# Half of the experts of a product-key FFN by one fetch per token instead of dense products, on one Trainium2 core

## The chip, the cores and the metric

The kernel runs on one core of one Trainium2 chip. The metric is the device time of one execution in microseconds. TensorE (PE) multiplies, VectorE (DVE) and ScalarE (ACT) work on tiles, GpSimd (POOL) and SyncE (SP) issue most DMAs. TensorE writes into PSUM, eight banks of 512 fp32 columns for each of 128 partitions.

## The reference

One decoder layer on 256 tokens of 1024 features: a sparse-attention and convolution mixer with residual, then a retrieval FFN. Only the FFN (peer_ffn) is touched. For each token and each of 8 heads it makes a query of two halves, scores 128 keys with each half, takes the top 16 of both, adds them in pairs, takes the top 16 pairs and a softmax g over these. A pair (i, j) is expert i*128 + j, of 16384:

```
a = gelu(einsum('bqhkd,bqd->bqhk', peer_u[expert], h2))
out = einsum('bqhk,bqhkd->bqd', g * a, peer_v[expert])
```

So each token uses 128 experts, each one a row of 1024 numbers in peer_u and one in peer_v. The result times gate2 is added to the residual.

## The kernel before, in words

The first 195 us (conditioning, mixer, output projection, second norm) end in h2, transposed (features on partitions), as two parts h2h and h2l, whose sum is h2. `split` (L116) makes such parts of a tile: a rounded copy on ScalarE (L117) and the rest on VectorE (L118). `mm3` (L120) multiplies two split operands in three passes (L121 to L123).

All weights come as tiles of 128x1024 (512 KB) through one queue in the order of use: `load` (L110) issues the DMA on SyncE, `advance` (L141) splits the tile, except those whose number is in `FULL`, which stay whole and are multiplied unsplit; `fill` (L156) keeps two tiles ahead. Rows of the gate2 conditioning (w_ada, 5) are put between V tiles 16 to 72 (L336).

The FFN is dense in the experts. `retrieve` (L805) first makes the queries (16 tiles) and their scores, with `stage1` top-16 rounds between them, then pairs, top 16 and softmax. It is a generator: after each piece it yields a cost, and the loop over U tiles draws pieces up to `BUDGET` a tile (L1002). `u_tile` (L960) multiplies the 128 experts of one j with all 256 tokens (8 calls of mm3, 256 columns) and takes the gelu on ScalarE. The first 64 (J0) run beside `retrieve`. The next 64 run beside `g_tile` (L975): for four tokens a step, ScalarE makes a one-hot of i (L981, L984) and VectorE one of j times g (L982); their product on TensorE (L986) is the gate of each (i, j), which is multiplied into B (L993). Then 128 V tiles: B's tile for j (split, `wh` and `wl`) times the tile of V, 12 matmuls of 512 columns into four output banks (L1020); last, `finish` multiplies with gate2, adds the residual and stores.

In the FFN VectorE's order is the order written (`manual_schedule`, L998); the other engines' order is the scheduler's.

Of the kernel before, what the change touches and what calls it, by code (L numbers as in the profile page):

```python
# [21 lines left out]
H = 8  # L22
# [13 lines left out]
# Order of the work. Streamed tiles are counted in the order in which they are used.  # L36
# [10 lines left out]
J0 = 64  # L47


def layout(a):  # L50
    """Only moves data: transposes, slices and repeats of the inputs."""
# [31 lines left out]
    o["pu"] = a["peer_u"].reshape(128, 128, KD, 128).transpose(1, 3, 2, 0)  # L83
    o["pv"] = a["peer_v"].reshape(128, 128, D).transpose(1, 0, 2)
# [7 lines left out]
def body(tc, i, out):  # L92
# [8 lines left out]
    his = pool("his", 3)  # L101
    los = pool("los", 3)
# [38 lines left out]
    def advance():  # L141
        pump(1)
        raw, use = loaded.pop(0)
        if use is not None:
            use(raw)
            return
        count[0] += 1
        if count[0] in FULL:
            ahead.append((raw,))
            return  # L150
        hi = his.tile([128, D], F32R, name="hi")
        lo = los.tile([128, D], F32R, name="lo")
        split(hi, lo, raw)
        ahead.append((hi, lo))
# [89 lines left out]
    def fold(col, acc, g):  # L244
        """Adds the sums of half of acc over its partitions to a column vector."""
# [23 lines left out]
    def normed(tb):  # L269
        """x times its reciprocal root mean square, tokens on partitions."""  # L270
# [52 lines left out]
    W += [(i["pu"][j].rearrange("p k c -> p (k c)"), None) for j in range(NJ)]  # L323
# [12 lines left out]
    for j in range(NJ):  # L336
        if j >= 16 and j % 8 == 0 and j < 80:
            k = (j - 16) // 8
            queue.append((i["w_ada"][5, k], add_row(gate2, k)))
        queue.append((i["pv"][j], None))  # L340
# [454 lines left out]
    B0 = pool("B0").tile([128, NJ // 2, L], F32, name="B0")  # L795
    tr = pool("tr")
    gw = pool("gw", 2)
    Ti = tr.tile([128, L], F32, name="Ti")
    Tj = tr.tile([128, L], F32, name="Tj")
    Tg = tr.tile([128, L], F32, name="Tg")  # L800
    p2 = ExitStack()
    r1 = p2.enter_context(tc.tile_pool(name="r1", bufs=1))
    r2 = p2.enter_context(tc.tile_pool(name="r2", bufs=2))

    def retrieve():  # L805
        skT = r1.tile([128, 16, 128], F32, name="skT")
        nc.scalar.dma_start(out=skT, in_=i["sk"])
        v16 = [r1.tile([128, 16, 16], F32, name=f"v16{tb}") for tb in range(NT)]
        x16 = [r1.tile([128, 16, 16], U32, name=f"x16{tb}") for tb in range(NT)]

        def top16(items, tag):
            """items: (values, sorted values out, positions out); chains run side by side."""
            ws = []
            for c, v, x in items:
                nc.vector.max(out=v[:, 0:8], in_=c)
            yield 0.4
            for c, v, x in items:
                nc.vector.max_index(out=x[:, 0:8], in_max=v[:, 0:8], in_values=c)
            yield 0.4
            for n, (c, v, x) in enumerate(items):  # L820
                w = r2.tile([128, c.shape[-1]], F32, name=f"{tag}{n}")
                nc.vector.match_replace(out=w, in_to_replace=v[:, 0:8], in_values=c, imm_value=NEG)
                ws.append(w)
            yield 0.4
            for w, (c, v, x) in zip(ws, items):
                nc.vector.max(out=v[:, 8:16], in_=w)
            yield 0.4
            for w, (c, v, x) in zip(ws, items):
                nc.vector.max_index(out=x[:, 8:16], in_max=v[:, 8:16], in_values=w)
            yield 0.4  # L830

        def stage1(hp, sg):
            return top16([(sg[:, tb], v16[tb][:, hp], x16[tb][:, hp]) for tb in range(NT)], "wv")

        def ready():
            while todo:
                yield from stage1(*todo.pop(0))

        def scores(hp, pqT):
            ps = p_acc.tile([128, NT, 128], F32, name="acc")  # L840
            for tb in range(NT):
                nc.tensor.matmul(ps[:, tb], pqT[:, tb * 128:tb * 128 + 128], skT[:, hp], start=True, stop=True)  # L842
            sg = r2.tile([128, NT, 128], F32, name="sg", bufs=10)
            nc.scalar.copy(sg, ps)
            todo.append((hp, sg))

        todo = []
        prev = None
        cur = iter(())
# [23 lines left out]
        yield 0  # L873
        yield from cur
        yield from ready()
        TB = range(NT)
        vv = [v16[tb].rearrange("p (h z) k -> p h z k", z=2) for tb in TB]
        xf = [r1.tile([128, 16, 16], F32, name=f"xf{tb}") for tb in TB]
        xv = [z.rearrange("p (h z) k -> p h z k", z=2) for z in xf]
        for tb in TB:  # L880
            nc.vector.tensor_copy(xf[tb], x16[tb])
        for tb in TB:
            nc.vector.tensor_scalar(xv[tb][:, :, 0], xv[tb][:, :, 0], 128.0, None, op0=OP.mult)
        yield 1.2
        cv = [r1.tile([128, H, NC2], F32, name=f"cv{tb}") for tb in TB]
        ce = [r1.tile([128, H, NC2], F32, name=f"ce{tb}") for tb in TB]
        o = 0
        a = 0
        while a < 16:
            nb = PAIRS[a]  # L890
            na = 1
            while a + na < 16 and PAIRS[a + na] == nb:
                na += 1
            for tb in TB:
                for c, s in ((cv[tb], vv[tb]), (ce[tb], xv[tb])):
                    dst = c[:, :, o:o + na * nb]
                    if nb == 1:
                        in0 = s[:, :, 0, a:a + na]
                        in1 = s[:, :, 1, 0:1].to_broadcast([128, H, na])
                    elif na == 1:  # L900
                        in0 = s[:, :, 0, a:a + 1].to_broadcast([128, H, nb])
                        in1 = s[:, :, 1, 0:nb]
                    else:
                        dst = dst.rearrange("p h (a b) -> p h a b", b=nb)
                        in0 = s[:, :, 0, a:a + na, None].to_broadcast([128, H, na, nb])
                        in1 = s[:, :, 1, None, 0:nb].to_broadcast([128, H, na, nb])
                    nc.vector.tensor_tensor(dst, in0, in1, op=OP.add)
            o += na * nb
            a += na
            yield 0.5  # L910
        tv = [r1.tile([128, H, 16], F32, name=f"tv{tb}") for tb in TB]
        tx = [r1.tile([128, H, 16], U32, name=f"tx{tb}") for tb in TB]
        for h in range(H):
            yield from top16([(cv[tb][:, h], tv[tb][:, h], tx[tb][:, h]) for tb in TB], "wc")
        tf = [r1.tile([128, H, 16], F32, name=f"tf{tb}") for tb in TB]
        gg = [r1.tile([128, H, 16], F32, name=f"gg{tb}") for tb in TB]
        gs = [r1.tile([128, H], F32, name=f"gs{tb}") for tb in TB]
        ef = [r1.tile([128, H, 16], F32, name=f"ef{tb}") for tb in TB]
        for tb in TB:
            nc.vector.tensor_copy(tf[tb], tx[tb])  # L920
            nc.vector.tensor_tensor(gg[tb], tv[tb], tv[tb][:, :, 0:1].to_broadcast([128, H, 16]), op=OP.subtract)
            nc.scalar.activation(out=flat(gg[tb]), in_=flat(gg[tb]), func=AF.Exp)
        yield 0.6
        for tb in TB:
            for h in range(H):
                for k in range(16):
                    ju = r2.tile([128, NC2], F32, name="ju")
                    nc.vector.scalar_tensor_tensor(ju, iota[:, :NC2], tf[tb][:, h, k:k + 1], ce[tb][:, h],  # L928
                                                   op0=OP.is_equal, op1=OP.mult,
                                                   accum_out=ef[tb][:, h, k:k + 1])  # L930
                    if k % 2:
                        yield 0.37
            nc.vector.tensor_reduce(out=gs[tb], in_=gg[tb], axis=AX.X, op=OP.add)
# [68 lines left out]
    for j in range(J0):  # L1002
        u_tile(j, 0)
        left += BUDGET
        while left > 0:
            left -= next(gen, 99.0)
# [66 lines left out]
```

## Time and profile before

| | us |
|---|---|
| median of 3 runs (lowest, highest) | 1032.94 (1032.71, 1033.36) |
| span of the profiled execution | 1031.9 |
| TensorE busy | 991.0 |
| VectorE busy | 774.2 |
| ScalarE busy | 595.9 |
| moved by DMA | 191.82 MB |

The profiled execution has no time of its own besides its span, first to last instruction. Busy time of TensorE counts matmuls whose ends are modelled. An fp32 matmul that is not split shows as two records.

### The profile page before, as it was taken

The page shows a single profiled execution, that of the slowest core. Times are in us where ns is not written, and L with a number is a line of the kernel's source. Part 1 is how long each engine was busy: PE and PEld are TensorE (multiplying, and loading weights), DVE is VectorE, ACT ScalarE, POOL GpSimd, SP SyncE. Part 2 cuts the span into 40 slices and gives each one's busy share as a digit, 9 for nine tenths or more (in the row PEclk, how much of TensorE's full clock was granted, in tenths as well). Part 3 has the DMA queues.
Part 4 walks back from the last instruction along what each step waited for, and adds up shares of the span by engine and source line. Part 5 has one row for each costly group of instructions (what it writes and reads, how often), then busy time and mean ns, then how long its engine had stood idle before and what let it go on. Part 6 is the DMA issues. An engine that isn't in the chain of part 4 may idle for free.

```text
span 1031.9 us, 18401 instructions
## 1 busy us (share of the span) xinstructions
PE 991.0 (96%) x6642; PEld 912.4 (88%) x6642; DVE 774.2 (75%) x2103; ACT 595.9 (58%) x1210; POOL 7.5 (1%) x20
## 2 busy tenths in 40 slices
PE   2599989999999999999999999999999999999998
PEld 2599987899999999999999999988888888888886
DVE  5789687788988999777788888866666666665655
ACT  3354643545445454599888888845454455455452
POOL 1000000000000000000000000000000000000000
PEclk9799998999999999999999999999999999999999
DMA  9686486345655655544444444456677777665663
GB/s 317 223 311 222 171 277 211 98 144 155 181 183 176 190 180 185 184 144 134 141 138 143 144 143 136 136 180 207 214 216 218 210 223 222 202 189 180 198 191 121
DMA packets 52891, 191.82 MB, mean 186 GB/s; under 512 B 6112, under 2 KB 6144, under 8 KB 52672
## 3 DMA queue, kind: packets, MB, share of 16 engines
q1 hardware_dynamic: 52416, 189.30, 58.4%
q8 instruction: 52, 0.85, 0.3%
q10 hardware_dynamic: 144, 1.05, 0.3%
q0 software_dynamic: 240, 0.31, 0.1%
q14 instruction: 39, 0.32, 0.1%
HBM read 189.58 MB, written 1.05 MB: 185 GB/s over the span
## 4 chain that ended last, share of the span: by engine, by line
PE 93%; DVE 4%; DMA 1%; ACT 1%; issue 0%; SPq 0%; ACTq 0%; DVEq 0%
PE acc L121 14%; PE acc L123 14%; PE acc L122 14%; PE mm L121 13%; PE mm L122 13%; PE mm L123 13%; PE pg L986 6%; PE acc L632 2%; DMA raw<-in_w_ada_dram 1%; DVE gate L219 1%; PE acc L842 1%; PE pg L517 1%; DVE acc L219 0%; PE mm L708 0%; ACT hi L117 0%
## 5 line engine op out<-in xcount | busy, mean ns | idle before, releaser
L118 DVE TENSOR_TENSOR lo<-raw,hi 128x1024 fp32r<-128x1024 f32 x302 | 369.1, 1223 | 122.7 <-ACT hi L117 120.3
L117 ACT CAST hi<-raw 128x1024 fp32r<-128x1024 f32 x302 | 316.0, 1047 | 158.1 <-PE mm L122 105.3
L121 PE MATMUL mm<-h2h,hi 128*128 128x256 f32 x1152 | 333.0, 289 | 0.5 <-ACT hi L117 0.4
L122 PE MATMUL mm<-h2l,hi 128*128 128x256 f32 x1152 | 325.9, 283 | 0.0
L123 PE MATMUL mm<-h2h,lo 128*128 128x256 f32 x1152 | 325.8, 283 | 0.0
L121 PEld LDWEIGHTS mm<-h2h,hi 128*128 128x128 f32 x1152 | 220.7, 192 | 0.9 <-ACT hi L117 0.9
L122 PEld LDWEIGHTS mm<-h2l,hi 128*128 128x128 f32 x1152 | 221.0, 192 | 0.0
L123 PEld LDWEIGHTS mm<-h2h,lo 128*128 128x128 f32 x1152 | 220.5, 191 | 0.0
L121 PE MATMUL acc<-hi,wh 128*128 128x512 f32 x512 | 199.7, 390 | 0.0
L123 PE MATMUL acc<-hi,wl 128*128 128x512 f32 x512 | 199.3, 389 | 0.0
L122 PE MATMUL acc<-lo,wh 128*128 128x512 f32 x512 | 199.3, 389 | 0.0
L117 ACT CAST wh<-B 128x256 fp32r<-128x256 f32 x128 | 52.0, 407 | 148.4 <-PE acc L122 145.6
L122 PEld LDWEIGHTS acc<-lo,wh 128*128 128x128 f32 x512 | 96.1, 188 | 20.1 <-issue 0.2
L123 PEld LDWEIGHTS acc<-hi,wl 128*128 128x128 f32 x512 | 96.1, 188 | 20.0
L121 PEld LDWEIGHTS acc<-hi,wh 128*128 128x128 f32 x512 | 96.1, 188 | 20.0 <-issue 0.2
L118 DVE TENSOR_TENSOR wl<-B,wh 128x256 fp32r<-128x256 f32 x128 | 54.2, 424 | 52.4 <-ACT wh L117 51.8
L981 ACT ACTIVATE oi<-iota,Ti 128x128 f32<-128x128 f32 x256 | 88.0, 403 | 0.0
L993 DVE TENSOR_TENSOR B<-pg,B 128x256 f32<-128x256 f32 (+63 forms) x127 | 45.0, 355 | 46.3 <-PE pg L986 46.3
L982 DVE TENSOR_SCALAR oj<-iota,Tj,Tg 128x128 f32<-128x128 f32 x256 | 71.3, 342 | 1.6 <-PE pg L986 1.6
L986 PE MATMUL pg<-oj,oi 128*128 128x128 f32 x512 | 67.6, 275 | 0.0
L986 PEld LDWEIGHTS pg<-oj,oi 128*128 128x128 f32 x512 | 62.8, 192 | 0.0
L928 DVE SCALAR_TENSOR_TENSOR ju<-iota,tf,ce 128x50 f32<-128x50 f32 x256 | 51.7, 266 | 0.0
(220 smaller groups left out, 945.9 us busy)
## 6 DMA issues: line engine op xcount, KB each, us to landing
raw<-in_pu_dram SPq DMA_DIRECT2D x128, 512.0 KB, 3.7
raw<-in_pv_dram SPq DMA_DIRECT2D x128, 512.0 KB, 4.3
raw<-in_w_ada_dram SPq DMA_DIRECT2D x48, 512.0 KB, 5.0
raw<-in_wq_dram SPq DMA_DIRECT2D x16, 512.0 KB, 3.7
raw<-in_w_c_dram SPq DMA_DIRECT2D x12, 512.0 KB, 4.7
raw<-in_w_kv_dram SPq DMA_DIRECT2D x8, 512.0 KB, 5.9
raw<-in_w_out_dram SPq DMA_DIRECT2D x8, 512.0 KB, 5.0
raw<-in_w_iq_dram SPq DMA_DIRECT2D x4, 512.0 KB, 4.8
```

Source lines behind the costliest of these rows:

```text
L117: nc.scalar.copy(hi, src)
L118: nc.vector.tensor_tensor(lo, src, hi.bitcast(F32), op=OP.subtract)
L121: nc.tensor.matmul(ps, a[0], b[0], start=first, stop=False)
L122: nc.tensor.matmul(ps, a[0], b[1], start=False, stop=False)
L123: nc.tensor.matmul(ps, a[1], b[0], start=False, stop=last)
L219: nc.vector.scalar_tensor_tensor(acc[:, s], raw[:, s], sc[:, k:k + 1], acc[:, s], op0=OP.mult, op1=OP.add)
L632: nc.tensor.matmul(ps[0], w[0][:, s], hT[:, k], start=k == 0, stop=k == KD - 1)
L928: nc.vector.scalar_tensor_tensor(ju, iota[:, :NC2], tf[tb][:, h, k:k + 1], ce[tb][:, h], op0=OP.is_equal, op1=OP.mult, accum_out=ef[tb][:, ...
L981: nc.scalar.activation(out=oi[:, n], in_=iota, func=AF.Square, bias=Ti[:, t:t + 1])
L982: nc.vector.tensor_scalar(oj[:, n], iota, Tj[:, t:t + 1], Tg[:, t:t + 1], op0=OP.is_equal, op1=OP.mult)
L986: nc.tensor.matmul(ps[:, n], oi[:, n], oj[:, n], start=True, stop=True)
L993: nc.vector.tensor_tensor(B[:, :m, t], pv[:, j0:j0 + m], B[:, :m, t], op=OP.mult)
```

## The change

- The tiles of U and V for j < 64 stay dense, but whole (`WHOLE`): each product is one unsplit fp32 matmul, against h2f, the fp32 sum of h2h and h2l made on GpSimd. B keeps only j < 64, and the gate product has 64 columns.
- The experts with j >= 64 come by fetch: U and V rows lie side by side in one array `uv` (8 KB a row). For each token GpSimd issues one indirect DMA by the list of its 128 experts, into a buffer of 128 partitions; an index with j < 64 has 65536 added, is out of bounds and is not moved. Nine such buffers are there (`ring`): three share the pool of split weights, six are new.
- Tokens go in quads, one from each strip of 32 partitions. h2 is transposed back to rows (`rows_of_h2`), split. For a token a matmul over its strip of 32 rows (`tile_position`) with one column of the identity, repeated 128 times, spreads its row of h2 over 128 partitions in PSUM; VectorE multiplies it with the fetched U rows and sums (two tokens and half of the features a turn, four turns a quad). After gelu and gate, `strips` multiplies the four tokens' coefficients with the fetched V rows, in column strips of 32, into the same output banks as the dense V tiles. Then the next fetch is issued.
- The pieces are laid between the dense matmuls by `run`, a budget in us. Retrieval goes one block of 128 tokens at a time; the lookup of the expert is three operations on 16x50 elements in place of 256 small ones, with the middle one on GpSimd for the first block. `g_step` staggers the gate product over three tiles, and after the U tiles it runs on until all 64 groups are done.
- All engines' order is now the order written. The gate2 rows lie between U tiles 4 to 18.

```diff
+WHOLE = set(FULL) | set(range(53, 53 + 2 * J0))
+ROWS = tuple(range(4, 20, 2))
...
+    nc.gpsimd.tensor_tensor(h2f, h2h.bitcast(F32), h2l.bitcast(F32), op=OP.add)
...
+        for tb in TB:
+            for g in range(2):
+                pt = p_g.tile([128, 4, 128], F32, name="pg")
+                for z in range(4):
+                    nc.tensor.transpose(pt[:, z], h2f[:, g * 4 + z, TS[tb]], ident)
+                s = slice(g * 512, g * 512 + 512)
+                split(h2r[0][:, tb, s], h2r[1][:, tb, s], flat(pt))
...
+    def stream():
+        yield from cur
+        while todo:
+            yield from stage1(*todo.pop(0))
+        yield from retrieve(0)
+        yield from retrieve(1)
+        state["R"] = True
+        yield 0.1
+        yield from pairs()
...
+    def run(us):
+        spent[0] += us
+        while spent[0] > 0:
+            z = next(gen, None)
+            if z is None:
+                spent[0] = 0.0
+                return
+            spent[0] -= z
...
+        for k in range(KD):
+            nc.tensor.matmul(ps, w[0][:, k * 128:k * 128 + 128], h2f[:, k], start=k == 0, stop=k == KD - 1)
+            if k % 4 == 3:
+                run(1.75)
...
+    def ring():
+        n = state["row"] = state.get("row", -1) + 1
+        if n % RINGS == 0:
+            return halves.tile([128, 2 * D], F32, name="uv", tag="hl")
+        return uvp.tile([128, 2 * D], F32, name="uv")
...
+    def fetch():
+        n = state["quad"] = state.get("quad", -1) + 1
+        if n >= L // 4:
+            return
+        rows = []
+        for q in range(4):
+            t = n // 32 * 128 + q * 32 + n % 32
+            rows.append(ring())
+            nc.gpsimd.indirect_dma_start(
+                out=rows[q], out_offset=None, in_=i["uv"],
+                in_offset=bass.IndirectOffsetOnAxis(ap=iv[:, t:t + 1], axis=0),
+                bounds_check=128 * 128 - 1, oob_is_err=False)
+        quads.append(rows)
+
+    def strips(n, z, rows):
+        tb = n // 32
+        c = n % 32
+        parts[tb] -= 1
+        for d in range(2):
+            for q in range(4):
+                nc.tensor.matmul(po[tb][d][q * 32:q * 32 + 32], z[:, q, 31 - c:63 - c],
+                                 rows[q][:, D + d * 512:D + d * 512 + 512],
+                                 start=False, stop=not parts[tb], tile_position=(0, q * 32))
+        spent[0] += 1.72
+        fetch()
+
+    def pairs():
...
+            while len(po) <= tb:
+                yield 1e6
+            rows = quads.pop(0)
+            ah = wa2.tile([128, 2, 4], F32, name="ah")
+            for q0 in (0, 2):
+                for d in range(2):
+                    ds = slice(d * 512, d * 512 + 512)
+                    bs = spreads[turn % len(spreads)]
+                    turn += 1
+                    for part in range(2):
+                        for x in range(2):
+                            p = slice((q0 + x) * 32, (q0 + x) * 32 + 32)
+                            t = (q0 + x) * 32 + c
+                            nc.tensor.matmul(bs[x], pick[p, t:t + 1].to_broadcast([32, 128]), h2r[part][p, tb, ds],
+                                             start=part == 0, stop=part == 1, tile_position=((q0 + x) * 32, 0))
+                    for x in range(2):
+                        nc.vector.tensor_tensor_reduce(out=junk, in0=rows[q0 + x][:, ds], in1=bs[x], scale=1.0,
+                                                       scalar=0.0, op0=OP.mult, op1=OP.add,
+                                                       accum_out=ah[:, d, q0 + x:q0 + x + 1])
+                    if q0 == 2 and d == 0 and wait is not None:
+                        strips(*wait)
+                        wait = None
+                    spent[0] += 0.45
+                    yield 1.55
+            z = zs[n % len(zs)]
+            ge = wa2.tile([128, 4], F32, name="gx")
+            nc.vector.tensor_tensor(ge, ah[:, 0], ah[:, 1], op=OP.add)
+            nc.scalar.activation(out=ge, in_=ge, func=AF.Gelu_apprx_tanh)
+            nc.vector.tensor_tensor(z[:, :, 31], ge, gp[:, tb * 128 + c:tb * 128 + 128:32], op=OP.mult)
+            yield 0.4
+            wait = (n, z, rows)
+        strips(*wait)
...
+    for j in range(J0):
+        ps = u_tile(j)
+        if late is not None:
+            evict(late)
+        late = ps
+        g_step()
+        if state.pop("R", False):
...
+            po.append([p_acc.tile([128, 512], F32, name="acc") for _ in range(2)])
+            clear(po[0])
+            spreads.append([p_acc.tile([128, 512], F32, name="acc") for _ in range(2)])
+            fetch()
+            fetch()
+    evict(late)
+    while spread[0] < L:
+        g_step()
+        run(1.0)
+    row_done(gate2)
+    po.append([p_mm.tile([128, 512], F32, name="mm") for _ in range(2)])
+    clear(po[1])
+    spreads.append([p_g.tile([128, 512], F32, name="pg") for _ in range(2)])
+    spent[0] = 0.0
+
+    def v_tile(j):
+        v = take()
+        fill(min(AHEAD, J0 - 1 - j))
+        for tb in TB:
+            parts[tb] -= 1
+            for d in range(2):
+                nc.tensor.matmul(po[tb][d], B0[:, j, TS[tb]], v[0][:, d * 512:d * 512 + 512],
+                                 start=False, stop=not parts[tb])
+            run(1.72)
```

The charges of the other pieces: a `stage1` round 5 x 0.4; `retrieve` 0.6, seven times 0.3, then for each pair of heads 5 x 0.4, 0.1, twice 0.9 (first block) or 1.8 (second), and 0.9 for each sum, last 0.3, 0.8, 1.0 and 0.4; `evict` and `g_step` take 0.35, 0.35 and 1.1 from the budget.

## Rows read from the trace of the kernel before

**Rows 1.** The page, part 1: busy time, share of the span, instructions.
```profile
PE 991.0 (96%) x6642; PEld 912.4 (88%) x6642; DVE 774.2 (75%) x2103; ACT 595.9 (58%) x1210; POOL 7.5 (1%) x20
```
**Rows 2.** The page, part 4: chain of waits by engine.
```profile
PE 93%; DVE 4%; DMA 1%; ACT 1%; issue 0%; SPq 0%; ACTq 0%; DVEq 0%
```
**Rows 3.** Windows by stage: length, busy time of each engine, clock, DMA share, GB/s.
```profile
196.00:252.00 56.00, 55.54 (x465) 55.03 (x465) 44.58 (x166) 27.35 (x51) 0.00 (x0) 1.00 0.52 158
252.00:436.00 184.00, 183.94 (x1533) 183.55 (x1532) 163.60 (x874) 92.99 (x149) 0.00 (x0) 1.00 0.59 181
436.00:675.00 239.00, 239.00 (x2033) 239.00 (x2032) 191.88 (x501) 210.54 (x566) 0.00 (x0) 1.00 0.46 141
675.00:1027.00 352.00, 351.94 (x1557) 290.80 (x1555) 221.47 (x272) 175.54 (x258) 0.00 (x0) 1.00 0.66 199
```
**Rows 4.** Groups by line and shape: the splits of weight tiles.
```profile
L118 DVE TENSOR_TENSOR lo<-raw,hi 128x1024 fp32r<-128x1024 f32 x302 | 369.1, 1223 | 122.7 <-ACT hi L117 120.3
L117 ACT CAST hi<-raw 128x1024 fp32r<-128x1024 f32 x302 | 316.0, 1047 | 158.1 <-PE mm L122 105.3 <-DMA raw<-in_pv_dram 20.6 <-DVE ju L928 12.7
```
**Rows 5.** Chain in order of time, unsplit fp32 matmuls: start, us, two records each.
```profile
99.76 3.45 PE acc L632 x16
...
435.93 0.89 PE pg L986 x8
...
940.86 1.72 PE mm L708 x4
```
**Rows 6.** Timeline of the V stage, two matmuls in turn: start, duration.
```profile
1014.76 0.39 PE L122 MATMUL acc<-lo,wh 128*128 128x512 f32 x1
1014.99 0.39 PE L123 MATMUL acc<-hi,wl 128*128 128x512 f32 x1
```
**Rows 7.** Timeline around four attention scores of 64 rows.
```profile
106.60 0.28 PE L123 MATMUL acc<-h1h,lo 128*128 128x256 f32 x1
...
106.81 0.70 PE L491 MATMUL pg<-kT,qT 64*128 64x256 f32 x4
...
107.35 0.60 PE L491 MATMUL mm<-kT,qT 64*128 64x256 f32 x4
...
107.88 0.39 PE L121 MATMUL acc<-h1h,hi 128*128 128x256 f32 x1
```
**Rows 8.** Groups on VectorE: products read from PSUM.
```profile
L1028 DVE TENSOR_TENSOR raw<-acc,gate 128x512 f32<-128x512 f32 x4 | 2.8, 692 | 0.7 <-PE acc L123 0.7
...
L492 DVE CUSTOM_DVE_ANT_0 ml<-pg,mb 128x256 f32<-128x256 f32 x4 | 1.5, 421 | 0.9 <-PE pg L491 0.9
```
**Rows 9.** GpSimd's queue, L747 (4 KB) and L214 (256 KB), and DMA's highest window.
```profile
DMA to landing us min/median/max: 3.4/3.4/3.4
...
aow<-in_aow_dram POOLq DMA_DIRECT2D x1, 256.0 KB, 6.9
...
4.00:10.00 6.00, 0.00 (x0) 0.00 (x0) 1.30 (x2) 3.37 (x9) 1.54 (x3) 1.00 1.05 381
```
**Rows 10.** Groups on VectorE: three of the operations of a first-stage round.
```profile
L818 DVE FIND_INDEX8 x<-v,sg 128x8 uint32<-128x128 f32 x32 | 8.7, 285 | 0.0
...
L815 DVE MAX8 v<-sg 128x8 f32<-128x128 f32 x32 | 7.5, 277 | 0.0
...
L818 DVE MATCH_VALUE_LOAD x<-v,sg 128x8 f32 x32 | 2.4, 74 | 0.0
```
**Rows 11.** Line 842, the scores of the queries: first and last start.
```profile
L842 PE MATMUL acc<-skT,pqT x64: 270/275/377, 202.5 to 251.6; 128*128 128x128 f32 x64
```
**Rows 12.** Timeline of one gate step on ScalarE, and a small product.
```profile
437.07 1.27 ACT L981 ACTIVATE oi<-iota,Ti 128x128 f32<-128x128 f32 x4
...
438.37 0.63 ACT L984 ACTIVATE oi<-oi 128x512 f32<-128x512 f32 x1
...
441.03 0.16 DVE L973 TENSOR_TENSOR B<-B,ge 128x4 f32<-128x4 f32 x1
```

More of the change, by code (lines that the diff above doesn't have):

```diff
@@ L100, in body @@
     raws = pool("raws", 3)
[L101 to L102 removed]
+    halves = pool("halves", 3)
     p_acc = pool("p_acc", 4, space=PSUM)
@@ L335, in body @@
     assert not ada
[L336 to L339, printed above, removed]
+    for j in range(J0):
+        if j in ROWS:
+            queue.append((i["w_ada"][5, ROWS.index(j)], add_row(gate2, ROWS.index(j))))
+        queue.append((i["pu"][j].rearrange("p k c -> p (k c)"), None))
+    for j in range(J0):
         queue.append((i["pv"][j], None))
@@ L792, in body @@
     p1.close()
-    B0 = pool("B0").tile([128, NJ // 2, L], F32, name="B0")
+    TB = range(NT)
+    order = ExitStack()
+    order.enter_context(tc.manual_schedule())
+    B0 = pool("B0").tile([128, J0, L], F32, name="B0")
     tr = pool("tr")
     gw = pool("gw", 2)
+    h2f = tr.tile([128, KD, L], F32, name="h2f")
     Ti = tr.tile([128, L], F32, name="Ti")
@@ L803, in body @@
     r2 = p2.enter_context(tc.tile_pool(name="r2", bufs=2))
[L805 to L847, printed above, removed]
@@ new lines, in stage1, with scores, queries @@
+    def stage1(hp, sg):
+        return top16([(sg[:, tb], v16[tb][:, hp], x16[tb][:, hp]) for tb in TB], "wv")
+    def scores(hp, pqT):
+        ps = p_acc.tile([128, NT, 128], F32, name="acc")
+        for tb in TB:
+            nc.tensor.matmul(ps[:, tb], pqT[:, tb * 128:tb * 128 + 128], skT[:, hp], start=True, stop=True)
+        sg = r2.tile([128, NT, 128], F32, name="sg", bufs=10)
+        nc.scalar.copy(sg, ps)
+        todo.append((hp, sg))
+    todo = []
+    cur = iter(())
+    def queries():
+        nonlocal cur
@@ new lines, in body, with summed @@
+    pend = []
+    def summed(keep):
+        while len(pend) > keep:
+            e, eq = pend.pop(0)
+            nc.vector.tensor_reduce(out=e, in_=eq, axis=AX.X, op=OP.add)
+            yield 0.9
+    def stream():
[5 more added lines that the diff above has]
+        state["R"] = True
+        yield 0.1
+        yield from pairs()
+    state.clear()
+    queries()
+    rows_of_h2()
@@ L961, in u_tile @@
+    gen = stream()
+    spent = [0.0]
+    def run(us):
[6 more added lines that the diff above has]
+            spent[0] -= z
+    evicted = [0]
+    spread = [0]
+    stage = [None, None]
+    groups = [0]
+    def u_tile(j):
         w = take()
@@ L1007, in body, with finish @@
+    def finish(tb, d):
+        s = slice(d * 512, d * 512 + 512)
+        tmp = raws.tile([128, D], F32, name="raw")[:, :512]
+        nc.vector.tensor_tensor(tmp, po[tb][d], gate2[:, s], op=OP.mult)
+        nc.vector.tensor_tensor(tmp, xs[:, tb, s], tmp, op=OP.add)
+        nc.sync.dma_start(out=out[tb * 128:tb * 128 + 128, s], in_=tmp)
+    for j in range(J0):
+        v_tile(j)
     for _ in gen:
         pass
-    p2.close()
+    for tb in TB:
+        for d in range(2):
+            finish(tb, d)
```

340 lines of the change are left out of this document (180 added, 160 removed).

## The prediction

> **What bounds the kernel now.** Read first is the busy share of each engine: TensorE 96%, VectorE 75% [rows 1]. Then the chain of waits, which is TensorE for 93% of the span [rows 2]. Then busy time by stage: in the queries (196 to 252 us), the first 64 U tiles (252 to 436), the second 64 with the gate matrices (436 to 675) and the V tiles (675 to 1027) TensorE has no gap at a granted clock of 1.00, while VectorE, ScalarE and the DMA engines have room [rows 3]. So from 252 us on the time is the number of TensorE passes and nothing else. A U tile is 184/64 = 2.88 us (24 passes of 256 columns, 0.12 us each), a V tile 352/128 = 2.75 us (12 passes of 512 columns, 0.228 us each [rows 6]). The 302 splits on VectorE and ScalarE are large (369 and 316 us [rows 4]) but lie beside it; removing them gains nothing by itself.
>
> **What the dense half costs now.** An unsplit fp32 matmul of 256 columns takes 3.45/8 = 0.43 us, one of 512 columns 1.72/2 = 0.86 us, and four of 128 columns 0.89 us [rows 5] (each leaves two records). So 64 U tiles of 8 matmuls: 64 x 3.45 = 221 us. The gate products halve to 64 columns: 0.45 us a group. 64 V tiles of 4 matmuls: 64 x 3.44 = 220 us.
>
> **What a quad of tokens costs TensorE.** Spreads: 4 turns of 4 split matmuls of 512 columns. The two row strips of a turn write different banks; that two row strips run together is shown by the attention scores: 8 records, four fp32 matmuls of 64 rows and 256 columns, fit between 106.81 and 107.88 us, where one after the other they would need 4 x 0.43 = 1.73 [rows 7]. So a turn is 2 x 0.228 = 0.45 us, a quad 1.8. V strips: 8 fp32 matmuls of 512 columns, in column strips of 32. No row of before shows column strips. One behind the other they are 8 x 0.86 = 6.9 us, four together 1.72; I take 1.72, because two row strips do overlap. The Trainium skill (TensorE: Matmul & The Clock Gate, "Measured speedup vs the span model") has four row strips at 3.07 times and three column strips at 2.38 times, not 4 and 3; as an estimate at 3.07 the eight would be 2.24 us and the total some 33 us more. No row here has four strips to set beside it. Changing from full array to strips and back also costs: from the last full matmul at 106.60 to the next one at 107.88 are 1.28 us; less its own 0.12 and two overlapped pairs of 0.43 each, 0.30 us are left [rows 7]. That is 0.15 us a change.
>
> **Where the quads run.** The side stream is paid out by a budget. I followed its payments in program order: six waiting first-stage rounds and the first retrieval end behind U tile 11, the second at the last half of tile 31, with 0.85 us of budget left. The stream then goes on to the quads, finds no output bank yet and charges 1,000,000 us; the budget is reset only ahead of the V stage. So no quad lies in the U stage: all 64 lie in the V stage, 256 turns behind 116 of its 128 half tiles, the last strips behind V tile 57. 53 groups of gates have been started by the end of the U stage.
>
> **The cycle of a quad, the main term.** Row buffers are nine. Rows 1, 2 and 3 of quad n+2 (and row 0 of n+3) wait for the buffers that the V strips of quad n free. A fetch moves on average 62.6 of 128 rows (the reference's own selection: 62.6 of 128 experts a token have j>=64), 8 KB each: 0.51 MB. The way from the end of one quad's strips to the next one's: semaphores 0.2; the fetch of row 1; two reductions, which free the banks; the next spread into these banks, 0.45; the strips queued behind that spread, 1.72; two changes of mode, 0.3. TensorE takes its matmuls in order, so dense V work behind a waiting spread waits too.
> Fetch: no row shows an indirect fetch. A 4 KB load by GpSimd's queue in a quiet stretch landed after 3.4 us; 256 KB behind others after 6.9 [rows 9]. Moving 0.51 MB at the highest rate seen, 381 GB/s [rows 9], adds 1.35. Bounds 3.4 and 6.9; I take 3.4 + 1.35 = 4.75. The Trainium skill (DMA: Bandwidth & Descriptors, "Anatomy of one DMA — SWDGE (gpsimd) path") has 2.0 us plus bytes at 436 GB/s for this path, as an estimate 3.2 us a fetch. The trace disagrees as far as it goes: its 4 KB took 3.4.
> Reduction of 512 columns from PSUM: 0.69 us for the plain product of that size [rows 8], 0.42 for the same operation on 256 columns. Two: 1.38 us.
> Cycle: 0.2 + 4.75 + 1.38 + 0.45 + 1.72 + 0.3 = 8.8 us. The engines alone would allow less: TensorE per quad 1.8 + 1.72 + 58 x 3.44/64 = 3.1 of dense work + 0.8 of changes (116 stays x 0.30 and 64 x 0.27 more for the strips, over 64) = 7.4; VectorE 8 x 0.69 + 0.7 for two small products at 0.16 [rows 12] with the trip over ScalarE between them (an estimate) = 6.2; the DMA engines 4 x 1.35 + 0.9 x 1.38 = 6.6.
>
> **The sum**, on the profiled execution's span of 1031.9 us (the runs' median 1032.94 lies 1.0 us above it, which I add):
> - up to the last score of the queries, 251.9 [rows 11], unchanged
> - rows of h2: 16 fp32 transposes at 0.222 = 3.6, and 1 for the evictions into two banks: 256.5
> - U stage: 221 + 53 x 0.45 = 245: 501.5
> - TensorE waits for the transposes of the first retrieval, because a first-stage round is charged 2.0 us, but two chains of five VectorE operations of 0.23 to 0.27 us busy, with their loads, are some 3.0 [rows 10]: 8 (bounds 0 and 15). Clearing two banks, behind the GpSimd zeroing: 4. Together 513.5
> - remaining 11 groups of gates, at ScalarE's pace of 1.27 + 0.63 = 1.9 us [rows 12], nothing beside them: 21, and 2 to drain: 536.5
> - sum of gate2 over partitions and two more banks: 1.72 + 0.6 + 1.72 = 4: 540.5
> - V stage: 64 x 8.8 = 563, and 6.4 V tiles without turns, 22: 1125.5
> - four results, 8 products at 0.69, and the last store: 6: 1131.5; with the 1.0 around the span 1132.
> Edits off this path: the new expert lookup on VectorE and GpSimd, the earlier gate2 rows (their DMAs on SP's queue lie in U tiles 4 to 18, at most one load more a tile against 3.45 us), the merged pool of halves (same depth). Hidden by TensorE's U tiles; without cover the lookup would cost the difference in VectorE time, a few us, inside the 0 to 15 above.
>
> **Rivals.**
> (1) Overlap as meant, faster: fetches hidden, changes of mode free because weights load ahead. Then a quad is 1.8 + 1.72 + 3.1 = 6.6, V stage 64 x 6.6 + 22 = 444, total 992. For: weights do load beside running matmuls, and two quads are asked for ahead of time. Against: 0.30 us of change [rows 7], 3.4 us for even 4 KB [rows 9]. It needs a fetch below 6.6 - 4.05 = 2.55 us.
> (2) Fetch hidden, changes not: 7.4 a quad, 496, total 1044, slower by 1%. It needs a fetch below 7.4 - 4.05 = 3.35 us, under the lower bound. The Trainium skill's rule for the fetch (the page above) leads to this rival, as an estimate.
> (3) Column strips one after the other: 5.2 us more a quad on the same path, 64 x 5.2 = 330: 1463. Against: the overlapped row strips.
> Not a rival but a bound: each fetch is spread over 16 engines unevenly; if it lands with its slowest, or when GpSimd's issue is slow, 5.7 instead of 4.75: V stage 61 more, 1193; at 6.9, 1270.
>
> **Chances.** Forecast (cycle bound by the fetch, 8 to 10 us a quad; own range 1075 to 1205) 0.53; rival 1 0.29; rival 2 0.12; rival 3 0.06. Most of the chance lies on both signs: rival 1 is kept high because its stage sum without waits is 76 us below today's (251.9 to 1026.3 is 774; 245 + 225 of quads + 220 + 9 is 699), so a small error in the fetch decides. The range 985 to 1205 takes rivals 1 and 2 for most of their spread and leaves rival 3 and slow fetches out. Faster by over 0.2% 0.29, within 0.2% (about what measurement of this kernel tells apart) 0.03, as part of rival 2, slower 0.68.
>
> **What would show it.** U tiles of 3.45 us without gaps, no spread ahead of the V stage, a stretch of some 20 us at ScalarE's pace between them. In the V stage, TensorE idle ahead of the spreads, released by VectorE reductions that were themselves released by the fetch; fetches landing 4 to 6 us after issue; 8.8 us from strips to strips; eight strips within 1.8 us. Wrong if the spreads never wait, if strips follow each other at 0.86 us, or if quads stand in the U stage.

## The result, and the profile after

The changed kernel takes 1250.9 us (median of four runs, 1246.8 to 1254.0); the kernel before, beside it, 1033.2 (1032.7 to 1033.5). The ratio is 1.211 (95% interval 1.207 to 1.214): slower, as forecast, but by 218 us and not by 99. The span of the profile is 1252.2.

The page of after, part 1 (engine, busy us, share of the span, instructions), to be set beside [rows 1]:
```profile
PE 1112.3 (89%) x5644; PEld 677.1 (54%) x5644; DVE 764.3 (61%) x2341; ACT 295.6 (24%) x808; POOL 293.1 (23%) x295
```
TensorE is busy for 121 us longer in all and still stands idle for 140 us, where it had 41 before. The windows of after by stage (length, busy time of each engine, granted clock, DMA share, GB/s): queries, U stage, last gate groups, V stage; they answer [rows 3]:
```profile
196.00:261.00 65.00, 58.36 (x466) 57.34 (x466) 46.94 (x165) 27.92 (x52) 4.51 (x1) 0.95 0.36 121
261.00:553.00 292.00, 276.01 (x1448) 243.90 (x1448) 170.49 (x667) 143.50 (x444) 36.26 (x27) 0.98 0.42 143
...
553.00:580.00 27.00, 23.61 (x109) 20.83 (x108) 15.59 (x58) 21.22 (x58) 0.00 (x0) 0.62 0.06 20
580.00:1226.00 646.00, 574.37 (x2521) 203.00 (x2520) 375.07 (x1152) 13.86 (x66) 244.25 (x247) 0.93 0.73 245
```
The stages are those forecast. GpSimd issues 247 of the 256 fetches in the V stage (244 of its us; the first nine, which fill the buffers, lie in the U stage), no spread stands ahead of 584.0 us, and the short stretch at ScalarE's pace is there. But the V stage, 563 + 22 us in the prediction, has 664 (from 582.1, where its first V product starts, to 1245.8).

What TensorE and VectorE wait for in the V stage of after (us in total, times, longest):
```profile
PE acc L1139 <- DVE ah L1142: 61.4, 60, 2.5
```
```profile
DVE junk L1142 <- DMA uv<-in_uv_dram,iv: 129.8, 102, 2.9
DVE junk L1142 <- PE acc L1139: 36.8, 30, 6.6
```
The chain is the one forecast: TensorE's spread waits for a reduction that frees its bank, and the reduction waits for a fetched row. The groups of the V stage (busy us, mean ns):
```profile
L1101 POOL DMA_INDIRECT uv<-in_uv_dram,iv x247 | 244.3, 989 | 537.6 <-PE acc L1113 320.6 <-PE mm L1113 121.5 <-DVE ah L1142 50.4
L1142 DVE CUSTOM_DVE_ANT_0 junk<-uv,pg 128x512 f32<-128x512 f32 x256 | 176.1, 688 | 62.2 <-PE pg L1139 13.9 <-PE acc L1139 12.6 <-DVE ah L1142 1.0
```
And one quad's middle in the timeline of after (start, us, engine, line, operation):
```profile
706.63 0.69 DVE L1142 CUSTOM_DVE_ANT_0 junk<-uv,acc 128x512 f32<-128x512 f32 x1 [0.79 <-DMA uv<-in_uv_dram,iv]
...
708.04 1.92 PE L1113 MATMUL acc<-uv,z 128*32 128x512 f32 x16
...
708.66 0.69 DVE L1142 CUSTOM_DVE_ANT_0 junk<-uv,pg 128x512 f32<-128x512 f32 x1
...
709.49 0.69 DVE L1142 CUSTOM_DVE_ANT_0 junk<-uv,acc 128x512 f32<-128x512 f32 x1
...
710.21 0.99 POOL L1101 DMA_INDIRECT uv<-in_uv_dram,iv  x1 [3.71 <-DVE ah L1142]
...
711.50 0.99 POOL L1101 DMA_INDIRECT uv<-in_uv_dram,iv  x1 [0.30 <-issue]
```
Eight V strips (16 records) lie within 1.92 us: four column strips do run together, so rival 3 is out. Reductions follow each other every 0.83 us, not 0.69. GpSimd gives 0.99 us to each issue and 0.30 between two, so rows 2 and 3 of a quad are asked for 1.3 and 2.6 us behind row 1. From the first strip of one quad to the first of the next are 9.93 us in the mean over 63 (median 9.43, the longest twentieth over 13.1); the prediction had 8.8.

By the stages of the sum, on the span:

| stage | predicted, us | measured, us | difference |
|---|---|---|---|
| start of U | 256.5 | 261.4 | +4.9 |
| U stage, with TensorE's wait in it | 245 + 12 | 291.6 | +34.6 |
| last gate groups, banks | 27 | 29.1 | +2.1 |
| V stage | 585 | 663.7 | +78.7 |
| finish | 6 | 6.4 | +0.4 |
| span | 1131.5 | 1252.2 | +120.7 |

### The profile page after: what moved, and what is told of

Same layout as the page of the kernel before. It is cut to its first block, busy times and chain, and to the rows that moved or that the text cites. A ratio compares the mean times of both kernels' runs of the same rounds, so it can differ in the third digit from the quotient of the medians.

```text
span 1252.2 us, 16661 instructions
## 1 busy us (share of the span) xinstructions
PE 1112.3 (89%) x5644; PEld 677.1 (54%) x5644; DVE 764.3 (61%) x2341; ACT 295.6 (24%) x808; POOL 293.1 (23%) x295
## 5 line engine op out<-in xcount | busy, mean ns | idle before, releaser
L1101 POOL DMA_INDIRECT uv<-in_uv_dram,iv x256 | 253.3, 989 | 540.2 <-PE acc L1113 320.6
L1142 DVE CUSTOM_DVE_ANT_0 junk<-uv,acc 128x512 f32<-128x512 f32 x256 | 176.0, 687 | 182.3 <-DMA uv<-in_uv_dram,iv 129.8
L1029 PE MATMUL mm<-h2f,raw 128*128 128x256 f32 x1024 | 237.3, 386 | 2.8 <-DMA raw<-in_pu_dram 2.4
L1142 DVE CUSTOM_DVE_ANT_0 junk<-uv,pg 128x512 f32<-128x512 f32 x256 | 176.1, 688 | 62.2 <-PE pg L1139 13.9
L1029 PEld LDWEIGHTS mm<-h2f,raw 128*128 128x128 f32 x1024 | 192.6, 193 | 30.0 <-issue 4.7
L1153 ACT ACTIVATE gx<-gx 128x4 f32<-128x4 f32 x64 | 13.1, 205 | 627.1 <-DVE gx L1152 528.2
L1139 PE MATMUL acc<-rh,pick 32*128 32x512 f32 x256 | 99.6, 507 | 64.7 <-DVE ah L1142 61.4
L1209 PE MATMUL acc<-raw,B 128*128 128x512 f32 x256 | 137.7, 664 | 0.0
L1209 PE MATMUL mm<-raw,B 128*128 128x512 f32 x256 | 137.0, 661 | 0.0
L1065 PE MATMUL pg<-oj,oi 128*128 128x64 f32 x512 | 72.5, 291 | 6.7 <-ACT oi L1077 6.7
L1139 PE MATMUL acc<-rl,pick 32*128 32x512 f32 x256 | 77.8, 438 | 0.0
```

Source lines behind the costliest of these rows:

```text
L1029: nc.tensor.matmul(ps, w[0][:, k * 128:k * 128 + 128], h2f[:, k], start=k == 0, stop=k == KD - 1)
L1065: nc.tensor.matmul(ps[:, n], oi[:, n], oj[:, n], start=True, stop=True)
L1101: nc.gpsimd.indirect_dma_start(out=rows[q], out_offset=None, in_=i["uv"], in_offset=bass.IndirectOffsetOnAxis(ap=iv[:, t:t + 1], axis=0), ...
L1139: nc.tensor.matmul(bs[x], pick[p, t:t + 1].to_broadcast([32, 128]), h2r[part][p, tb, ds], start=part == 0, stop=part == 1, tile_position=( ...
L1142: nc.vector.tensor_tensor_reduce(out=junk, in0=rows[q0 + x][:, ds], in1=bs[x], scale=1.0, scalar=0.0, op0=OP.mult, op1=OP.add, accum_out=a ...
L1153: nc.scalar.activation(out=ge, in_=ge, func=AF.Gelu_apprx_tanh)
```

## The experiments

Each ran once, beside a run of the kernel before on the same chip (1030.7 to 1034.1 us); where nothing else is said it is the changed kernel with one edit. "Cycle" is the mean from the first strip of a quad to the first of the next. Theory F: in the V stage the fetch and what hangs on it set the cycle. Its rival P: TensorE's and VectorE's own work do. In the code `...` stands for lines left out.

**No fetch.** The rows stand in fixed buffers of zeros:
```
-            rows.append(ring())
-            nc.gpsimd.indirect_dma_start(
-                out=rows[q], out_offset=None, in_=i["uv"],
...
+            rows.append(fixed[(4 * n + q) % 9])
```


> Leaves out every fetch: the quads read nine buffers of zeros that are written once, so all matmuls, reductions and products stay and no quad waits for rows. Theory F (a quad's cycle is bound by the fetch through the nine buffers, and the waits let TensorE's clock fall): the V stage falls from 664 us to 64 x 7.4 + 22 = some 495 to 520, the granted clock there rises from 0.93 to 1.00, total 1085 to 1110. Rival P (TensorE and VectorE themselves, with the changes of mode, make the cycle): strips to strips stay above 9 us, total above 1200.

1115.0 us, cycle 7.77. TensorE's waits and the window of the V stage:
```profile
PE acc L1136 <- DVE ah L1139: 8.6, 26, 0.6
```
```profile
580.00:1100.00 520.00, 508.94 (x2547) 185.34 (x2546) 373.83 (x1152) 13.15 (x64) 0.00 (x0) 1.00 0.20 62
```
The wait goes, TensorE is busy for 98%, and 136 us go with the fetch: theory F. But the waits are less than half of it. The V stages of after and of this run, whole:
```profile
582.10:1245.80 663.70, 592.07 (x2561) 210.70 (x2559) 377.44 (x1156) 13.15 (x64) 244.25 (x247) 0.93 0.72 240
579.90:1106.50 526.60, 515.54 (x2561) 188.00 (x2559) 376.30 (x1156) 13.15 (x64) 0.00 (x0) 1.00 0.19 62
```
Of the 137 us between them TensorE is idle for 60 more, and for 77 more it is busy with the same 2561 matmul records. In after 96 us of the stage lie at a granted clock of 0.5, here 3; at half speed those 93 us would, as an estimate, make up for at most 46 of the 77. What the other 31 are is not shown.

The run says more: even a fetch that costs nothing leaves the kernel 84 us slower than before. A quad costs TensorE itself 7.77 - 58 x 3.44/64 = 4.65 us, 298 us for all 64. The room that the change made for them was 774 - (U 221 + 58 of gate groups at 0.9 + V 220) = 275 us. The dense tiles dropped were worth more, 64 x (2.88 + 2.75) = 360 us; but the tiles kept, multiplied whole, went from 2.88 to 3.45 and from 2.75 to 3.44 us, and that gave 81 us back. So the quads cost less than the dense tiles that they replace; it is with the price of leaving the kept half unsplit that the change saves nothing on the engine that bounds the kernel.

**Narrow rows.** The same 256 fetches, of 512 bytes a row into the fixed buffers:
```
-            rows.append(ring())
+            rows.append(fixed[(4 * n + q) % 9])
             nc.gpsimd.indirect_dma_start(
-                out=rows[q], out_offset=None, in_=i["uv"],
+                out=rows[q][:, :128], out_offset=None, in_=i["un"],
```


> Same 256 indirect DMAs with the same lists and waits, but each row moves 512 B into its buffer instead of 8 KB; the rest of the buffers is zeros, so the products are not the reference's. Splits theory F. If moving the bytes is what makes the fetch long: rows land 3 to 4 us after issue, the cycle falls to 7.5 to 8, total 1090 to 1130. If issue on GpSimd (1.29 us a row) and fixed latency make it: cycle stays at 9 and more, total above 1200.

1119.5 us, cycle 7.84. The queue's row, before it and after it was narrowed:
```profile
q0 software_dynamic: 37104, 131.71, 32.0%
```
```profile
q0 software_dynamic: 8432, 8.60, 3.3%
```
GpSimd still issues for 246.6 us between 580 and 1100 us, and it costs 0.07 us a quad: GpSimd's issuing by itself is not what is dear. The run does not part the bytes from the wait for a buffer, though, since the waits are not the same as was expected. A narrow row touches only columns that the strips do not read. GpSimd's longest wait in the V stage of after, and in that of this run:
```profile
POOL uv L1101 <- PE acc L1113: 320.6, 30, 167.7
```
```profile
POOL fixed L1103 <- DVE ah L1144: 279.2, 83, 149.4
```
In this run it never waits for strips, and row 1 of quad n+2 is asked for 9.7 us before the strips of quad n start, where after asks 2.2 us behind their start (medians). What it does show is the fetch itself: a narrow row lands 2.4 us after issue in the median, and rows 2 and 3 no later after theirs (2.6 and 2.2), where whole rows take 4.95, 6.8 and 7.4.

**Strips early.** The strips of a quad stand behind the second turn of the next quad and not the third, so that buffers come free and fetches start one turn sooner:
```
-                    if q0 == 2 and d == 0 and wait is not None:
+                    if q0 == 0 and d == 1 and wait is not None:
```


> One position changed: the V strips of quad n are emitted after the second turn of quad n+1 instead of the third, so buffers come free earlier against the time their next rows are needed. Theory F: a quad's cycle falls by about one turn of reductions spread over the two quads of lead, to 8.1 to 8.6 undisturbed, total 1170 to 1210. Rival P: no change beyond 10 us, or slower, since TensorE then waits for the coefficients (VectorE, ScalarE, VectorE) ahead of the strips.

1158.4 us, cycle 8.47, better than expected. TensorE's waits for reductions before 1100 us fall from 51.0 and 1.9 us to:
```profile
PE acc L1139 <- DVE ah L1142: 9.9, 14, 1.7
PE pg L1139 <- DVE ah L1142: 2.8, 9, 0.4
```
Same bytes, same work, 92 us less: two thirds of what the fetch cost came from where the strips stood in TensorE's order. In the V stage 53 us of TensorE's idle time go and 43 of its busy time, with the time at a granted clock of 0.5 down from 96 to 17 us. That is theory F at its strongest, and it is the best kernel with the border at 64 up to here.

**Quads in the U stage.** The end of the stream's charge is mended, so that quads start beside U tiles:
```
-        yield 0.1
+        while not po:
+            yield max(spent[0], 0.0) + 0.1
```


> The side stream ends its turn when it finds no output banks, instead of charging 1,000,000 us, so quads are laid between U tiles 32 to 63 as well. Theory F: in the U stage a quad has longer between strips (some 14 us of U tiles and gates), so its fetch is hidden; about 20 quads move there, each adds some 4.3 us of TensorE work instead of a 10 us cycle: total 1190 to 1210. Rival P: TensorE's work is the same and only moved, total within 10 us of 1251.

1299.7 us, a miss. The U stage ends at 709 instead of 553, and a quad takes 12.0 us in the mean. In the U stage:
```profile
PE acc L1140 <- DVE ah L1143: 28.9, 40, 6.6
```
```profile
261.00:709.00 448.00, 398.01 (x1942) 291.24 (x1941) 258.31 (x956) 138.97 (x450) 95.49 (x87) 0.90 0.50 162
```
There only one pair of banks is free for spreads, so TensorE and VectorE take turns, and the U tiles behind a waiting spread wait too. That is inferred: the wait shown is 28.9 of the 156 us by which the U stage grows for the 15 quads in it, while the V stage falls by 122 (from 750.0 on). The charge of 1,000,000 us that the prediction found was no loss: it kept the quads out of a stage in which they are dearer.

**The add's line moved, and the gate groups.** First GpSimd's add for h2f moved down in the text alone:
```
-    nc.gpsimd.tensor_tensor(h2f, h2h.bitcast(F32), h2l.bitcast(F32), op=OP.add)
 ...
+            if hp == 4:
+                nc.gpsimd.tensor_tensor(h2f, h2h.bitcast(F32), h2l.bitcast(F32), op=OP.add)
```


> GpSimd's add that makes h2f is moved behind query head 4; all else as after the change. Theory (the add of two SBUF inputs slows the three VectorE splits that stand beside it at the start of the queries): the splits take about 3.5 us again instead of 7.83 us, U starts 3 to 5 us earlier, the time is 1244 to 1248. Rival (the splits are slow for a reason of their own, the add has no part in it): they still take 7 to 8 us and the time stays within 2 us of 1251.

1261.3 us, and the run tests nothing: GpSimd has no other work, so the add still starts at 193.8, as soon as h2l is there. Its work is that of the changed kernel, so its 10 us above the median of that one, and its cycle of 10.11 beside 9.93, say how far two runs of one kernel lie apart here; smaller differences between single runs tell nothing by themselves. The next run has this edit (as void there), the early strips, and more gate groups beside U tiles:
```
         g_step()
+        if j >= 32 and j % 2:
+            g_step()
```


> Strips early as in the run before (1158.4), the h2f add late, and a second gate group on every odd U tile from the 32nd on, so that all 64 groups are done when the U stage ends. Theory W (a gate group costs TensorE its weight loads, 0.9 us, wherever it stands): the U stage grows by some 11 x 0.9 = 10 us, the stretch of 24.5 us behind it goes, with the start of the queries 4 us less: 1134 to 1146. Rival (ScalarE's 1.9 us for the squares of a group sets the pace on these tiles too): the U tiles with two groups take over 5.5 us, the stretch is only moved, and the time is 1150 to 1160.

1147.9 us, 10.5 less than the early strips alone, which is no more than that spread, and between the two expected ranges. The stages are clearer: the U stage is 12.5 us longer than in the run before it for 11 groups more, 1.14 us each, and the stretch behind it is gone. Both theories had a part of it: a group costs more than its own 0.84 us, less than ScalarE's pace.

**The add made to wait, and small products of zeros.** The add stands behind a copy that reads a later result; and, read apart, two products of zeros of 128 columns in each quad of the V stage:
```
+            if hp == 4:
+                wt = r2.tile([128, 1], F32, name="wt")
+                nc.gpsimd.tensor_copy(wt, prev[:, :1])
+                nc.gpsimd.tensor_tensor(h2f, h2h.bitcast(F32), h2l.bitcast(F32), op=OP.add)
 ...
+                    if q0 == 2 and d == 0:
+                        for w in range(2):
+                            nc.tensor.matmul(po[tb][w][:, :128], zero, xs[:, 0, :128], start=False, stop=False)
```


> Two edits in two stages, read apart. (a) GpSimd's add now stands behind a small copy that reads the result of query head 4, so that it really runs later (in the run with the line moved it ran at the same place, 193.8 us, and the splits still took 7.83 us, so that run told nothing). Theory: the three splits at the start of the queries take about 3.5 us again and TensorE's wait for them (5.1 us) goes. Rival: still 7 to 8 us. (b) In each quad two products of zeros of only 128 columns (0.22 us each at full clock) ahead of the third turn's spread, in place of the one of 512 columns that left the cycle at 10.1. Theory C (low clock is dear): cycle 9.2 to 9.6, time 1205 to 1235. Rival (low clock only accompanies the waits): cycle 9.8 to 10.3, 1245 to 1265.

(a) The splits at the start of the queries, and the add, first in after and then in this run:
```profile
196.53 7.83 DVE L122 TENSOR_TENSOR hl<-raw,hl 128x1024 fp32r<-128x1024 f32 x3 [0.17 <-ACT hl L121]
...
196.49 4.51 POOL L819 TENSOR_TENSOR h2f<-h2h,h2l 128x2048 f32<-128x2048 f32 x1 [48.38 <-DVE h2l L122]
```
```profile
194.45 3.50 DVE L122 TENSOR_TENSOR hl<-raw,hl 128x1024 fp32r<-128x1024 f32 x3 [0.17 <-ACT hl L121]
...
212.61 4.61 POOL L891 TENSOR_TENSOR h2f<-h2h,h2l 128x2048 f32<-128x2048 f32 x1
```
Shown: beside GpSimd's add of two SBUF inputs the three splits take 7.83 us, away from it 3.50, as in before; the 4.33 us more are nearly the add's own length. TensorE's wait for them falls from 5.1 to 0.8 us, the clock of 0.5 that followed for 6.8 us does not appear, and U starts at 252.5, of which 2.1 us came from ahead of the splits. (b) 1266.5 us, cycle 10.25: no gain; see the next run.

**One product of zeros of 512 columns** in each quad, at the place where TensorE waits:
```
+                    if q0 == 2 and d == 0:
+                        for w in range(1):
+                            nc.tensor.matmul(po[tb][w % 2], zero, xs[:, 0, :512], start=False, stop=False)
```


> After the change, with one more 128x512 product of zeros by x into the output bank (it adds nothing; 0.86 us of TensorE at full clock) in each quad, put where TensorE waits anyway, ahead of the third turn's spread. Theory C (TensorE stands idle at that wait, the granted clock falls to 0.5 behind it for 101 us of the V stage, and that is dear, 0.54 us for each us): the time at half clock falls below 45 us, the mean from strips to strips from 9.93 to 9.1 to 9.4, the time is 1200 to 1225. Rival (the low clock is harmless, since the fetch sets the cycle; the product is only more work): the cycle stays at 9.9 or grows, 1250 to 1300.

1265.2 us. The time at half clock from V's start on, its last stretch counted whole, falls from 101 to 67 us; the cycle goes from 9.93 to 10.12, no more than the spread of two runs. What theory C, that the low clock is itself dear, had forecast did not come. In after the 25 cycles that touch a stretch at clock 0.5 take 11.0 us in the mean and the 38 others 9.21; but four runs with this order of the V stage (two of them with products of zeros) and 67, 101, 118 and 132 us at half clock have cycles of 10.12, 9.93, 10.25 and 10.11. Which comes first, the low clock or the long wait, stays open: the product itself may cost between 0 and 0.86 us a quad, and what the clock gave back can lie inside that.

**The border at 32, strips late.** 32 U and 32 V tiles; the quads start behind the U stage, among the gate groups, with 12 buffers. The budget's charge is mended as above:
```
-J0 = 64
+J0 = 32
...
-RINGS = 3
+RINGS = 4
 ...
     while spread[0] < L:
         g_step()
-        run(1.0)
...
+        run(3.4)
```


> The border is 32 and not 64: 32 U tiles and 32 V tiles are left to the dense way, 95.8 rows a token are fetched on average instead of 62.6 (201 MB instead of 131 MB), the ring has 12 buffers, the quads start right behind the U stage beside the gate groups, with the V tiles among them. Theory F (a quad costs its own fetch and its own TensorE work, the dense tiles are dear beside it): U ends near 410, then 64 quads of 9 to 10 us: 990 to 1060. Rival (the fetch of a row grows with its bytes, as the mean of the traffic at 245 GB/s of the V stage has it: 3.14 MB a quad is 12.8 us): 64 x 12.8 = 819 behind 410, that is 1230 and no gain.

1051.8 us, cycle 9.54. **The same with strips early:**

> As the border of 32, and the strips of a quad behind the first two turns of the next quad instead of the third, so that the next fetch is issued earlier; the h2f add late. Theory F: 5 us less for the start of the queries, and 0.5 to 1.4 us a quad less where the fetch still ends last: 940 to 1030, at any rate below the run with strips late. Rival (with 95.8 rows the DMA engines themselves are full, so an earlier issue lands no earlier): within 10 us of that run, by the queries' start alone.

1046.8 us, cycle 9.44; before was 1034.1 beside both. Its windows from the U stage's end on:
```profile
410.00:560.00 150.00, 131.60 (x593) 64.79 (x592) 98.03 (x342) 43.23 (x124) 70.60 (x67) 0.62 0.82 303
...
700.00:850.00 150.00, 144.00 (x668) 53.70 (x668) 100.95 (x313) 3.49 (x17) 69.58 (x71) 0.94 1.00 398
850.00:1000.00 150.00, 141.21 (x633) 51.44 (x632) 94.84 (x292) 3.29 (x16) 63.26 (x65) 0.93 0.98 390
```
With more fetching the kernel is 110 us faster than the early strips at 64. The likely reason is that each tile dropped saves TensorE 3.45 us on U and on V (221 us for 32), while a quad needs the same matmuls whatever the border; but the ring and the place of the quads changed too, so no run shows it alone. From 700 us on the DMA engines have no room (shares of 0.98 and 1.00 at 390 to 398 GB/s), and the gain of 5 us fits the rival, in which an earlier issue lands no earlier ("within 10 us"). Between 410 and 700 us, where gate groups and quads run without dense tiles, the granted clock is 0.60 to 0.62. Two products of zeros a quad in that stretch:
```
+                    if q0 == 2 and d == 0 and spread[0] < L:
+                        for w in range(2):
+                            nc.tensor.matmul(po[tb][w % 2], zero, xs[:, 0, :512], start=False, stop=False)
```


> The border of 32 with early strips (1046.8, 256 us of it at half clock between 410 and 713, where gate groups and quads run without dense tiles), with two 128x512 products of zeros in each quad of that stretch, ahead of the third turn's spread. Theory C: the granted clock of the stretch rises from 0.61 to 0.8 or more, its quads go from 10.5 to about 9.3 us, the time is 1005 to 1030, below the kernel before the change. Rival (the low clock there costs nothing, or two more products of 0.86 us, 1.72 at half clock, cost what it gives): 1045 to 1090.

1076.6 us:
```profile
410.00:560.00 150.00, 129.00 (x590) 58.80 (x589) 87.52 (x309) 39.56 (x113) 65.12 (x62) 0.78 0.76 280
```
The clock rises to 0.78, close to the 0.8 expected, and the stretch still grows by 31 us (the last gate group ends at 731.7 instead of 700.7): the rival. The products of its 28 quads are 48 us by themselves at full clock, so the run does not tell what the clock gave back. **The border at 48**, with these products and 9 buffers:

> The same with the border at 48 (80.6 rows a token, 169 MB, ring of 9 buffers): U ends at 464; behind it TensorE has 48 V tiles of 3.45 (166 us), 64 quads of some 4.7 (301 us) and 37 gate groups of 0.9 (33 us), 500 us, the DMA engines 169 MB at the 390 GB/s of the run before (433 us) and 25 MB of V. Theory (TensorE's own work is the bound between 32 and 64, with waits and clock of 10 to 20 per cent on it): 1015 to 1070. Rival (a cycle of 8.5 us as with the border of 64 and early strips is the floor of a quad, V tiles hidden in it): 464 + 64 x 8.5 + 20 = 1028, and 9.4 as with the border of 32: 1086.

1204.4 us, a clear miss. The last 16 U tiles and the first quads fall together: the first spread starts at 414.4 and the U stage ends at 572.8 instead of some 464. As with the quads in the U stage, only one pair of banks serves the spreads there (again inferred). Behind 573 us more is lost, and 15 V tiles remain when the quads are done at 1144; no run shows why. No version here beats the kernel before.

## Why the prediction was wrong

- **What bounds the kernel** held: TensorE without gaps from 252 us on [rows 3].
- **The mechanism of the slowdown** held: all quads in the V stage, the fetch ahead of the reductions ahead of the spreads, TensorE idle there. The runs without fetch and with early strips show it. What it left out is that idle time is only 60 of the 137 us that go with the fetch.
- **The step that failed is the cycle of a quad**, mis-sized at 8.8; it measured 9.93, and 63 x 1.13 = 71 of the 78.7 us of the V stage. By means of the 62 cycles of after that have a fetch, which add up, all three parts of the way were short: 2.35 us from the first strip to the issue of row 1, for 1.72 + 0.2; 5.15 for the fetch, for 4.75; 2.48 from there to the next strips, for 1.38 + 0.45 + 0.3 = 2.13. The typical cycle is nearer (median 9.43); the other 0.5 is the mean over the median, which I never had in the sum.
- **The long cycles** are those that touch a stretch at half clock: 25 of the 63, and they hold 55 of the 71 us. Row 1's fetch is hardly longer in them (5.24 us against 5.09 in the mean), TensorE stands idle for 0.76 us more, and the rest of their 1.8 us is time in which it counts as busy. The sum had TensorE at full clock throughout. That the low clock makes these cycles long is not shown; it may only follow the waits.
- **Luck in the fetch.** 4.75 was 3.4, the landing of a small load, and 1.35 for the bytes. A narrow row lands after 2.4 us, so as an estimate the bytes take some 2.5 of the median of 4.95: two errors that nearly cancel. The Trainium skill's rule for the fetch (DMA: Bandwidth & Descriptors, "Anatomy of one DMA — SWDGE (gpsimd) path") would give, as an estimate, 3.2 us; the trace disagrees: 4.95 in the median.
- **The engines' own bound** was low too: 7.77 and not 7.4.
- **Gate products**: 0.45 us a group was taken, half of [rows 5], since the columns are halved. A group in after:
```profile
355.28 1.00 PE L1065 MATMUL pg<-oj,oi 128*128 128x64 f32 x8
356.12 3.67 PE L1029 MATMUL mm<-h2f,raw 128*128 128x256 f32 x16
```
0.84 us to the start of the next U tile, as much as 128 columns took before; in tiles without a wait a U tile with a group is 4.35 us. That is 53 x 0.45 = 24 of the 34.6 us. Each group still loads eight times 128x128 weights. That these loads set the 0.84 is inferred from it, not shown by a run.
- **TensorE's wait for the first transposes**, 8 predicted in 0 to 15: there, 9.6 us of wait and some 13 lost:
```profile
PE acc L974 <- DVE fi L963: 9.6, 1, 9.6
```
The 13 hold part of a stretch at a granted clock of 0.5, from 310.0 to 320.2 us. The rest of the U stage's excess is smaller: waits for ScalarE's squares (3.3 us) and for loads (2.4), and another 3.4 us at 0.5.
- **The rows of h2**: sized for TensorE only. GpSimd's add was counted nowhere, and it made VectorE's splits late. A step taken off the critical engine was priced at nothing without asking what it shares.
- **The last groups** at ScalarE's pace held: 29.1 for 27 with the banks.
- **Rivals.** 3 fell with the strips' 1.92 us. 2 asked for 7.4 a quad; with no fetch at all it is 7.77. 1 (992) fails at its stage sum: 699 us had gate groups at half their price and quads without changes of mode, and the run without fetch gives 1115. So no outcome faster than before was to be had from this change at this border, whatever the fetch cost; 0.29 for it was too much. The 699 also lie 75 us below today's 774, not 76.
- **The range** (985 to 1205) left slow fetches out at the top, though the prediction itself worked out 1270 for 6.9 us: the bound of an operation that no row shows was known and not kept.

## What to carry to other kernels

When a change swaps dense work for fetched work, first count what the new work costs on the engine that bounds the kernel now, and what the change does to the work that stays: here 298 us of strips and spreads stood in for 360 us of dense products, but multiplying the kept half unsplit cost 81 us more, and everything else came on top. In a ring of buffers the time of a cycle runs from the instruction that frees a buffer, so the place of that instruction in its engine's order can be worth much of what the transfers cost (92 of 136 us here). And a cycle with a transfer on it was longer in the mean than in the median (9.93 and 9.43); a sum of typical durations gives the median at best.

## What the runs showed of the hardware

- Four column strips of 32 run together in fp32: eight products of 512 columns within 1.92 us, where one after the other they would need 6.9.
- An fp32 product of 64 columns is hardly cheaper than one of 128 when each brings new weights: 0.84 and 0.89 us for four.
- An indirect fetch by GpSimd costs 0.99 us of its time to issue and 0.30 to the next; 0.51 MB lands 4.95 us after issue as the first of a burst, the next three 6.8, 7.4 and 8.0 us after theirs (medians); the same rows cut to 512 bytes land after 2.2 to 2.6.
- GpSimd's add of two SBUF inputs slows VectorE's splits beside it from 3.50 to 7.83 us for three.
- Moving GpSimd's add down in the text moved nothing while GpSimd had no other work (it started at 193.8 us all the same); a dependency moved it, to 212.6.
